# A mixture-of-experts stage: TensorE in program order, an overflow piece folded earlier, one product for a slot's token and weight

## The chip, the cores and the metric

The kernel runs on one core of a Trainium2 chip. Its engines are TensorE (PE in the profile, with PEld for the loading of its stationary operand), VectorE (DVE), ScalarE (ACT), GpSimd (POOL) and SyncE (SP). The metric is the device time of one execution in microseconds, lower is better; several executions are run and the median is taken.

## The reference

The model has two layers on 512 tokens of width 1024. Each layer has two attention mixers and a SwiGLU block. The block of the first layer is dense; that of the second is a mixture of 8 experts, two for each token:

```python
logits = (h @ w_router).astype(jnp.float32)
top_val, top_idx = lax.top_k(logits, TOP_K)            # TOP_K = 2, 8 experts
top_w = jax.nn.softmax(top_val, axis=-1)
combine = jnp.sum(jax.nn.one_hot(top_idx, N_EXPERTS) * top_w[..., None], axis=-2)
for e in range(N_EXPERTS):
    out = out + combine[..., e:e + 1] * swiglu(h, w_gu_e[e], w_dn_e[e])   # 1024 -> 2 x 1408 -> 1024
```

All is in float32. Only the expert block of the second layer is touched by the change.

## The kernel before

**Precision.** Each float32 operand of the large products is split into a high part (rounded) and a low remainder: for weights, ScalarE makes `ehi` (L1468) and VectorE subtracts it to give `elo` (L1469). A product then is three products on TensorE: high by high, high by low, low by high.

**The experts.** `moe` (L1706) runs the 8 experts one after the other. An expert has 128 slots for its tokens; where it got more, up to 64 more are kept as an overflow. The first expert to run is expert 0; the others follow in an order by their counts that is worked out on the chip (`rank`, L1228). With these inputs two of the eight have an overflow: the first and the fifth to run. All that belongs to an overflow stands under a branch, `self.over(e)`, that each engine takes or not by the expert's count.

**One expert**, `expert_blocks` (L1552), is a generator that is stepped once per k. It has four gate/up pieces u = 0 to 3 of 352 columns (8 k each, 6 products a k: L1647, L1648) and three down pieces d = 0 to 2 (11 k each, 3 products a k: L1681 to L1683). The loop counts them as (u, k) with u = 0 to 3 for gate/up and 4 to 6 for down. Around them stand, at places given by constants: the evacuation of a gate/up piece (`evac_gu`: Silu on ScalarE, a product on VectorE), the transposes of the activation (`tr`, L1577, then `ah` by L1581 and `al` by L1582), the weight splits (`SN`), and the scatter of the previous expert's rows (`rest`, at ER0).

**The overflow of an expert.** Ahead of each gate/up piece 32 products of the overflow rows (L1627, here called an overflow piece) go to two PSUM banks. They are folded by `ov_gu(u)`: two ScalarE copies (L1549), two VectorE adds (L1550), a Silu (L1590), a product (L1591). `OV` = 5 is the k of the pieces 0 to 2; the last is folded in the down piece d = 0 at `OV3` = 6. At `OT` = 8 the results are transposed (`ov_tr`, L1598) and split into `aot` (L1601, L1602), and behind d = 0 come 66 overflow down products (L1695, L1696).

**The slots of the next expert** are prepared meanwhile by `prep_a`, a generator too. It makes four one-hot matrices of tokens by slots (`one_hots`, L1274, on POOL; on VectorE for the first expert), multiplies them by the token numbers (`slots`, L1289) and by the weights (`slot_weights`, L1307), turns these into `ix` and `w` and gathers the rows (L1501). `prep_b` (at PB, PB1) transposes and splits the gathered rows, `prep_over` those of the overflow. For the first expert, `prep_a` also runs the rest of the routing (`route_rest`, 26 small VectorE operations and an exponential).

**What sets the order.** ScalarE issues in program order, by an order region around the whole kernel. On the other engines the compiler's scheduler chooses a fixed order from its own estimates of time, with the program order as priority. An instruction that finds its operands not ready holds up all that stands behind it on its engine.

Of the kernel before, what the change touches and what calls it, by code (L numbers as in the profile page):

```python
# [43 lines left out]
ER = 11  # L44
EA = 4
ORDER = (7, 3, 4, 5, 0, 6, 1, 2)
P0 = (0, 2), (0, 6), (1, 1)
OV, OV3, OT, OY = 5, 6, 8, (5, 8)
ER0 = 3
LA = 2  # L50
SN = (2, 4, 6, 8), (2, 4, 6, 8), (2, 4, 6, 8), (2, 4, 6), (7, 8, 9, 10), (1, 4, 8), (1, 4, 8)
TU, TE = 5, 6
TD = 5
PA, PA1, PA2, PB, PB1, PO = (1, 2), (2, 0), (2, 4), (4, 2), (4, 7), (5, 4)
FD = 3
PINH = ()
BK = 0, 1, 2, 3, 4, 5, 6, 7
# [19 lines left out]
class Trunk:  # L77
# [1129 lines left out]
    def route_rest(self):  # L1207

        nc, rp = self.nc, self.rp

        def over_e(a):
            return a.unsqueeze(2).to_broadcast([P, NT, NE])

        e2, w1 = rp.tile([P, NT], F32, name="e2"), rp.tile([P, NT], F32, name="w1")
        nc.vector.tensor_sub(e2, self.m8[:, :, 1], self.m8[:, :, 0])
        nc.scalar.activation(e2, e2, AF.Exp)
        nc.vector.tensor_scalar_add(w1, e2, 1.0)
        nc.vector.reciprocal(w1, w1)
        nc.vector.tensor_mul(e2, w1, e2)
        nc.vector.tensor_sub(self.M, self.M, self.s1)  # L1220
        nc.vector.tensor_tensor(self.s1, self.s1, over_e(w1), op=ALU.mult)
        nc.vector.tensor_tensor(self.M, self.M, over_e(e2), op=ALU.mult)
        nc.vector.tensor_add(self.wt, self.s1, self.M)
        self.rank()
        self.cols = rp.tile([P, NT, NE, 3], BF16, name="cols")
        self.weight_cols(self.cols, self.wtr, rp.tile([P, NT, NE], F32, name="wrem"))

    def rank(self):  # L1228
# [40 lines left out]
    def one_hots(self, n, pos, q):  # L1269

        oh = []
        for t in range(NT):
            o = self.ex.tile([P, CAP], BF16, tag="oh", bufs=4, name=self.nm("oh"))[:, :n]
            i = q.tensor_scalar(o, self.iotas[:, :n], pos[:, t], None, op0=ALU.is_equal)  # L1274
            self.tc.keep_in_program_order(i)
            oh.append(o)
        return oh

    def slots(self, n, oh):

# [205 lines left out]
    def prep_a(self, e):  # L1486

        nc, ex = self.nc, self.ex
        o = ORDER[e]
        oh = self.one_hots(CAP, self.posr[:, :, o:o + 1] if e else self.pos[:, :, 0:1], nc.gpsimd if e else nc.vector)  # L1490
        yield
        sl, fin = self.slots(CAP, oh)
        self.sl = sl
        if e:
            wfin = self.slot_weights(oh, sl, self.cols[:, :, o], self.psl)
            yield
        fin()
        g = self.g = [ex.tile([P, D], F32, tag="xg0", bufs=1, name=self.nm("xg")), self.views[-1]]

        def get(j):  # L1500
            nc.gpsimd.indirect_dma_start(out=g[j], out_offset=None, in_=self.hd[:, :],  # L1501
                                         in_offset=bass.IndirectOffsetOnAxis(ap=sl[j][2], axis=0))

        get(0)
        if e == 0:
            self.counts()
        self.ne[e] = nc.values_load(self.cnti[0:1, o:o + 1] if e else self.cnti[0:1, NE:], min_val=0, max_val=S)
        with self.over(e):
            get(1)
        if e == 0:  # L1510
            yield
            self.route_rest()
            yield
            wfin = self.slot_weights(oh, sl, self.cols[:, :, o])
            yield
        wfin()

    def prep_b(self):

# [32 lines left out]
    def expert_blocks(self, e, sl, xs, xo):  # L1552
# [51 lines left out]
        def ov_y(d):  # L1604
            c = dcol(d)
            self.fold(yo[:, c], ops[d][:, :c.stop - c.start], yo[:, c])
            nc.vector.tensor_scalar_mul(yo[:, c], yo[:, c], sl[1][3])

        def evac_gu(u, pg, pu):
            c = slice(u * GC, (u + 1) * GC)  # L1610
            nc.scalar.activation(a[:, c], pg, AF.Silu)  # L1611
            nc.vector.tensor_mul(a[:, c], a[:, c], pu)  # L1612
# [5 lines left out]
        last = None  # L1618
        for u in range(DFE // GC):
            ws = self.e_next(KD // GK)  # L1620
            with self.over(e):  # L1621
                for k in range(KD):
                    hi, lo = ws[k // GK]
                    st, sp, kk = k == 0, k == KD - 1, k % GK
                    for w, s0, s1 in ((hi, st, False), (lo, False, sp)):
                        for g in range(2):
                            nc.tensor.matmul(og[g], xo[:, k], w[:, g, kk], start=s0, stop=s1)  # L1627
            if u:
                evac_gu(u - 1, *last)
            last = pg, pu = self.psa()[:, :GC], self.psa()[:, :GC]  # L1630
            for k in range(KD):
                yield u, k
                if (u, k) == (0, ER0) and self.rest:
                    self.rest()
                if k == OV and u < 3:
                    with self.over(e):
                        ov_gu(u)
                if k == TU:
                    trev = tr(u * GC // P)
                if k in SN[u]:  # L1640
                    self.e_split()
                if k == TE:
                    trev()
                hi, lo = ws[k // GK]
                st, sp, kk = k == 0, k == KD - 1, k % GK
                for x, w, s0, s1 in ((xh, hi, st, False), (xh, lo, False, False), (xl, hi, False, sp)):
                    nc.tensor.matmul(pg, x[:, k], w[:, 0, kk], start=s0, stop=s1)  # L1647
                    nc.tensor.matmul(pu, x[:, k], w[:, 1, kk], start=s0, stop=s1)  # L1648
            self.e_splits(SN[u].count(KD))
        evac_gu(u, *last)  # L1650
        dws = []
        for d in range(ND):
            if d == 0:
                dws.append(self.e_next(3))
            if d != 1:
                py = self.psa()
            pd, py = py[:, :dcol(d).stop - dcol(d).start], None
            for k in range(KE):
                yield 4 + d, k
                if d == 0 and k == TD:  # L1660
                    tr(KE)()
                if k in SN[4 + d]:
                    self.e_split()
                if d == 0 and k == OV3:
                    with self.over(e):
                        ov_gu(3)
                if d == 0 and k == OT:
                    with self.over(e):
                        ov_tr()
                if d and k == 1:  # L1670
                    evac_y(d - 1, last)
                if (4 + d, k) == OY:
                    with self.over(e):
                        for j in range(ND):
                            ov_y(j)
                        nc.gpsimd.indirect_dma_start(out=self.out[0],
                                                     out_offset=bass.IndirectOffsetOnAxis(ap=sl[1][2], axis=0),
                                                     in_=yo, in_offset=None, compute_op=ALU.add)
                hi, lo = dws[d][k // DK]
                kk = k % DK  # L1680
                nc.tensor.matmul(pd, ah[:, k], hi[:, 0, kk], start=k == 0, stop=False)  # L1681
                nc.tensor.matmul(pd, ah[:, k], lo[:, 0, kk], start=False, stop=False)  # L1682
                nc.tensor.matmul(pd, al[:, k], hi[:, 0, kk], start=False, stop=k == KE - 1)  # L1683
            last = pd
            if d == 0:
                py = self.psa()
                dws += [self.e_next(3) for _ in range(ND - 1)]
                ops.append(self.psa())
                with self.over(e):  # L1689
                    for j, ws in enumerate(dws):  # L1690
                        ps = ops[j][:, :dcol(j).stop - dcol(j).start]
                        for k in range(KE):
                            hi, lo = ws[k // DK]
                            kk = k % DK
                            nc.tensor.matmul(ps, aot[:, k], hi[:, 0, kk], start=k == 0, stop=False)  # L1695
                            nc.tensor.matmul(ps, aot[:, k], lo[:, 0, kk], start=False, stop=k == KE - 1)  # L1696
# [9 lines left out]
    def moe(self):  # L1706
# [19 lines left out]
            self.e_load()  # L1726
        self.hold = False
        next(pb)
        xo = self.prep_over(0)
        self.e_splits(1 + LA)  # L1730
        for e in range(NE):
            sl = self.sl
            for u, k in self.expert_blocks(e, sl, self.xs, xo):
                if e == 0 and (u, k) in P0:
                    next(pa, None)
                if e + 1 == NE:
                    continue
                if (u, k) == PA:
                    pa = self.prep_a(e + 1)
                if (u, k) in (PA, PA1, PA2):  # L1740
                    next(pa, None)
                if (u, k) == PB:
                    pb = self.prep_b()
# [74 lines left out]
    def whole(self):  # L1818
# [14 lines left out]
        with order:  # L1833
# [15 lines left out]
                self.route()  # L1849
            with experts:  # L1850
                self.moe_pools(experts)
                self.moe()
                with tc.issue_after(self.last_dve.ins):
                    self.overflow_list()
        with ExitStack() as experts:
# [29 lines left out]
```

## Time and profile before

| What | Value |
|---|---|
| median of 3 runs | 1715.91 us (1715.15 to 1716.56) |
| the profiled execution | 1717.1 us |
| its span, first to last instruction | 1715.3 us |
| mean granted clock of TensorE | 0.985 of full speed |
| TensorE busy | 1644.6 us |
| VectorE, ScalarE, GpSimd busy | 1094.1, 978.3, 206.4 us |

The busy times are those of the page of the profile, and an engine is busy while one of its instructions runs. The granted clock is that of TensorE as the chip allowed it; it has two levels, 2.4 GHz (1.00) and 1.2 GHz (0.50). The expert stage takes the last third of the span.

### The profile page before, as it was taken

To read this page: it belongs to the slowest core of one execution; us is meant where nothing else is said; L and a number is where in the kernel's file an instruction comes from. 1 tells how busy PE (TensorE), PEld (TensorE's weight loads), DVE (VectorE), ACT (ScalarE), POOL (GpSimd) and SP (SyncE) were. 2 spreads that over 40 slices of the span, in tenths; PEclk is the share of its full clock that TensorE was granted. 3 is DMA by queue.
4 is the path that set the end of the run, shared out by engine and by line. 5 is a ranking of instruction groups with operands and counts; after the bars stand their busy time and mean duration, and the time that the engine had idled before them with its cause. 6 is when DMAs were issued, how large, how long until landed. Compare 5 with 4: busy or idle time off the path is not lost. (4 is left out here: it accounts for less than half of the span.)

```text
span 1715.3 us, 26180 instructions
## 1 busy us (share of the span) xinstructions
PE 1644.6 (96%) x9031; PEld 1433.5 (84%) x9031; DVE 1094.1 (64%) x1844; ACT 978.3 (57%) x1750; POOL 206.4 (12%) x315
## 2 busy tenths in 40 slices
PE   6989999999999999999989999999899999999996
PEld 6867987788888888888868987887789999999996
DVE  5578678765533332336578678655667888767984
ACT  5666589754422222324667589643656776656773
POOL 6112100002000000000122000101012202102200
PEclk9999999999999999999999999999799999999998
DMA  6333333235333332443433333352959999869993
GB/s 179 108 86 101 80 98 80 76 103 177 99 99 96 95 94 91 134 130 99 111 83 103 93 86 80 102 186 100 309 190 302 299 363 353 300 211 342 313 345 87
DMA packets 270840, 273.73 MB, mean 160 GB/s; under 512 B 11424, under 2 KB 259232, under 8 KB 270688
## 3 DMA queue, kind: packets, MB, share of 16 engines
q1 hardware_dynamic: 255936, 230.98, 42.7%
q0 software_dynamic: 12288, 37.40, 8.0%
q10 hardware_dynamic: 2464, 3.41, 0.6%
q8 instruction: 85, 1.39, 0.3%
q14 instruction: 67, 0.55, 0.1%
HBM read 250.21 MB, written 13.14 MB: 154 GB/s over the span
## 5 line engine op out<-in xcount | busy, mean ns | idle before, releaser
L320 PE MATMUL mm<-b,whi 128*128 128x512 f32 x1072 | 426.4, 398 | 4.1 <-DVE b L534 3.3
L322 PE MATMUL mm<-b,wlo 128*128 128x512 f32 x1072 | 419.5, 391 | 0.0
L321 PE MATMUL mm<-b,whi 128*128 128x512 f32 x1072 | 419.1, 391 | 0.0
L297 DVE TENSOR_TENSOR wlo<-wr,whi 128x1024 fp32r<-128x1024 f32 (+1 forms) x176 | 213.1, 1213 | 208.3 <-ACT whi L296 206.3
L296 ACT CAST whi<-wr 128x1024 fp32r<-128x1024 f32 (+1 forms) x176 | 182.9, 1042 | 262.9 <-issue 120.5
L1469 DVE TENSOR_TENSOR elo<-er,ehi 128x1408 fp32r<-128x1408 f32 (+3 forms) x200 | 305.1, 1568 | 26.0 <-ACT ehi L1468 15.5
L1468 ACT CAST ehi<-er 128x1408 fp32r<-128x1408 f32 (+3 forms) x200 | 256.1, 1324 | 22.3 <-DVE oh L1274 5.5
L320 PEld LDWEIGHTS mm<-b,whi 128*128 128x128 f32 x1072 | 201.8, 188 | 45.2 <-DVE b L534 4.6
L322 PEld LDWEIGHTS mm<-b,wlo 128*128 128x128 f32 x1072 | 201.3, 188 | 42.6 <-DVE wlo L297 0.4
L321 PEld LDWEIGHTS mm<-b,whi 128*128 128x128 f32 x1072 | 201.8, 188 | 39.1 <-issue 0.2
L356 PE MATMUL mm<-whi,b 128*128 128x256 f32 x320 | 92.3, 289 | 1.7 <-DVE b L532 1.1
L357 PE MATMUL mm<-wlo,b 128*128 128x256 f32 x320 | 91.3, 285 | 0.4 <-DVE wlo L297 0.4
L358 PE MATMUL mm<-whi,b 128*128 128x256 f32 x320 | 91.0, 285 | 0.0
L1682 PE MATMUL pa<-elo,ah 128*128 128x352 f32 (+1 forms) x264 | 85.8, 325 | 2.7 <-PEq L1621 0.3
L1683 PE MATMUL pa<-ehi,al 128*128 128x352 f32 (+1 forms) x264 | 84.7, 321 | 3.3 <-DVE al L1582 3.3
L1681 PE MATMUL pa<-ehi,ah 128*128 128x352 f32 (+1 forms) x264 | 86.5, 328 | 0.9 <-PEq L1689 0.2
L1647 PE MATMUL pa<-ehi,xh 128*128 128x352 f32 x256 | 85.8, 335 | 0.0
L1648 PE MATMUL pa<-elo,xh 128*128 128x352 f32 x256 | 83.7, 327 | 2.0 <-PEq L1621 0.5
L1648 PE MATMUL pa<-ehi,xl 128*128 128x352 f32 x256 | 83.1, 325 | 0.9 <-PEq L1621 0.3
L1647 PE MATMUL pa<-elo,xh 128*128 128x352 f32 x256 | 83.1, 325 | 0.3 <-DVE elo L1469 0.3
L1647 PE MATMUL pa<-ehi,xl 128*128 128x352 f32 x256 | 83.2, 325 | 0.0
L1648 PE MATMUL pa<-ehi,xh 128*128 128x352 f32 x256 | 83.1, 325 | 0.0
(351 smaller groups left out, 3107.6 us busy)
## 6 DMA issues: line engine op xcount, KB each, us to landing
er<-in_w_gu_exp_dram SPq DMA_DIRECT2D x248, 352.0 KB, 6.5
wr<-in_w_in_dram SPq DMA_DIRECT2D x80, 512.0 KB, 3.9
wr<-in_w_gu_dense_dram SPq DMA_DIRECT2D x44, 512.0 KB, 3.8
er<-in_w_dn_exp_dram SPq DMA_DIRECT2D x32, 704.0 KB, 10.6
wr<-in_w_dn_dense_dram SPq DMA_DIRECT2D x20, 512.0 KB, 3.4
er<-in_w_dn_exp_dram SPq DMA_DIRECT2D x16, 640.0 KB, 9.0
er<-in_w_dn_exp_dram SPq DMA_DIRECT2D x16, 528.0 KB, 10.2
b<-b POOLq DMA_DIRECT2D x64, 128.0 KB, 2.8
```

Source lines behind the costliest of these rows:

```text
L296: self.nc.scalar.copy(hi, raw)
L297: self.nc.vector.tensor_sub(lo, raw, f32v(hi))
L320: self.nc.tensor.matmul(ps, hi[:, j], hh[j], start=st, stop=False)
L321: self.nc.tensor.matmul(ps, hi[:, j], hl[j], start=False, stop=False)
L322: self.nc.tensor.matmul(ps, lo[:, j], hh[j], start=False, stop=sp)
L356: nc.tensor.matmul(o, a, hi[:, j], start=first, stop=False, skip_group_check=True)
L357: nc.tensor.matmul(o, a, lo[:, j], start=False, stop=False, skip_group_check=True)
L358: nc.tensor.matmul(o, b, hi[:, j], start=False, stop=last, skip_group_check=True)
L1468: self.nc.scalar.copy(hi, raw)
L1469: self.last_dve = self.nc.vector.tensor_sub(lo, raw, f32v(hi))
L1647: nc.tensor.matmul(pg, x[:, k], w[:, 0, kk], start=s0, stop=s1)
L1648: nc.tensor.matmul(pu, x[:, k], w[:, 1, kk], start=s0, stop=s1)
```

## The change

It has four parts, all in the expert stage.

1. Inside `moe` TensorE too issues in program order (a nested order region); before, the scheduler chose.
2. For every expert after the first, `slots_all` takes the place of `slots` and `slot_weights`: `cols` gets two more columns with the token number's two parts, and one product of five columns gives index and weight of a slot. Two reductions of VectorE make `ix` and `w` from it.
3. The folding of the last overflow piece moves from d = 0, k = 6 to u = 3, k = 5, and the overflow transposes from d = 0, k = 8 to k = 3.
4. For the first expert, the rest of the routing is issued ahead of its first block. Its overflow rows are transposed at (0,2) instead of ahead of the block, with two weight splits; its first overflow piece follows at (0,4), and is folded at k = 7. Its slot weights come at (2,0) and (2,2). The steps of `prep_a` for the second expert come at (1,2), (2,2) and (2,5), and for the later ones at (0,6), (1,4) and (2,0), where all had (1,2), (2,0) and (2,4).

```diff
-P0 = (0, 2), (0, 6), (1, 1)
-OV, OV3, OT, OY = 5, 6, 8, (5, 8)
+P0 = (2, 0), (2, 2)
+EO = 2
+OV, OT, OY = 5, 3, (5, 8)
...
-PA, PA1, PA2, PB, PB1, PO = (1, 2), (2, 0), (2, 4), (4, 2), (4, 7), (5, 4)
+PA = ((1, 2), (2, 2), (2, 5)), ((0, 6), (1, 4), (2, 0))
+PB, PB1, PO = (4, 2), (4, 7), (5, 4)
...
-        self.cols = rp.tile([P, NT, NE, 3], BF16, name="cols")
+        self.cols = rp.tile([P, NT, NE, 5], BF16, name="cols")
+        for j in range(2):
+            nc.gpsimd.tensor_copy(self.cols[:, :, :, 3 + j], self.tokc[:, :, j:j + 1].to_broadcast([P, NT, NE]))
...
+    def slots_all(self, n, oh, cols):
+
+        nc, ps, res = self.nc, self.psy(), []
+        for b in range(0, n, P):
+            m = min(P, n - b)
+            o = ps[:m, (b // P) * 8:(b // P) * 8 + 5]
+            for t in range(NT):
+                nc.tensor.matmul(o, oh[t][:, b:b + m], cols[:, t], start=t == 0, stop=t == NT - 1)
+            res.append([b, m] + [self.ex.tile([P, 1], d, tag=g, bufs=4, name=self.nm(g))[:m]
+                                 for d, g in ((I32, "ix"), (F32, "w"))])
+
+        def fin():
+            for b, m, ix, w in res:
+                o = ps[:m, (b // P) * 8:(b // P) * 8 + 5]
+                with nc.allow_low_precision(reason="whole numbers below 512"):
+                    nc.vector.tensor_reduce(ix, o[:, 3:5], axis=AX.X, op=ALU.add)
+                nc.vector.tensor_reduce(w, o[:, 0:3], axis=AX.X, op=ALU.add)
...
-        sl, fin = self.slots(CAP, oh)
+        sl, fin = self.slots_all(CAP, oh, self.cols[:, :, o]) if e else self.slots(CAP, oh)
         self.sl = sl
         if e:
-            wfin = self.slot_weights(oh, sl, self.cols[:, :, o], self.psl)
             yield
...
-        last = None
-        for u in range(DFE // GC):
-            ws = self.e_next(KD // GK)
+        def mm_over():
             with self.over(e):
                 for k in range(KD):
                     hi, lo = ws[k // GK]
...
+        last = None
+        for u in range(DFE // GC):
+            ws = self.e_next(KD // GK)
+            if (e, u) != (0, 0):
+                mm_over()
             if u:
                 evac_gu(u - 1, *last)
             last = pg, pu = self.psa()[:, :GC], self.psa()[:, :GC]
             for k in range(KD):
                 yield u, k
+                if (e, u, k) == (0, 0, EO):
+                    xo = self.prep_over(0)
+                    self.e_splits(LA)
+                if (e, u, k) == (0, 0, EO + 2):
+                    mm_over()
                 if (u, k) == (0, ER0) and self.rest:
                     self.rest()
-                if k == OV and u < 3:
+                if k == (OV if e or u else KD - 1):
                     with self.over(e):
                         ov_gu(u)
...
-                if d == 0 and k == OV3:
-                    with self.over(e):
-                        ov_gu(3)
...
-        xo = self.prep_over(0)
-        self.e_splits(1 + LA)
+        xo = None
+        self.e_splits(1)
+        next(pa)
+        p0 = pa
         for e in range(NE):
             sl = self.sl
             for u, k in self.expert_blocks(e, sl, self.xs, xo):
                 if e == 0 and (u, k) in P0:
-                    next(pa, None)
+                    next(p0, None)
                 if e + 1 == NE:
                     continue
-                if (u, k) == PA:
+                at = PA[min(e, 1)]
+                if (u, k) == at[0]:
                     pa = self.prep_a(e + 1)
-                if (u, k) in (PA, PA1, PA2):
+                if (u, k) in at:
                     next(pa, None)
...
-                self.moe()
+                with tc.manual_schedule(engines={mybir.EngineType.PE}):
+                    self.moe()
```

## Rows read from the trace of the kernel before

**Rows 1.** The page, part 1: busy time of an engine.

```profile
PE 1644.6 (96%) x9031; PEld 1433.5 (84%) x9031; DVE 1094.1 (64%) x1844; ACT 978.3 (57%) x1750; POOL 206.4 (12%) x315
```

**Rows 2.** Stages: length, busy time by engine (instructions), PEclk, DMA share, GB/s.

```profile
1210.00:1703.00 493.00, 479.63 (x3082) 461.90 (x3082) 370.23 (x391) 315.58 (x341) 74.00 (x45) 0.98 0.88 292
1280.00:1290.00 10.00, 9.42 (x38) 8.57 (x38) 6.55 (x8) 5.95 (x8) 0.00 (x0) 0.50 0.36 102
1524.40:1534.40 10.00, 9.21 (x61) 8.66 (x62) 7.85 (x8) 9.29 (x11) 0.00 (x0) 1.00 0.41 114
```

**Rows 3.** TensorE's waits in the expert stage: us in total, times, longest.

```profile
PE py L1527 <- DMA xg<-hd,ix: 5.6, 1, 5.6
PE pa L1683 <- DVE al L1582: 3.3, 2, 2.1
...
PE mm L1695 <- DVE aot L1602: 1.4, 2, 0.8
...
PE py L1289 <- POOL oh L1274: 0.7, 2, 0.5
...
PE py L1540 <- DMA ao<-hd,ix: 0.6, 1, 0.6
...
PE pa L1647 <- DVE elo L1469: 0.3, 1, 0.3
```

**Rows 4.** TensorE's timeline, third expert: start, us, operation, count.

```profile
1376.60 0.69 PE L1289 MATMUL py<-tokc,oh 128*128 128x1 bf16 x16
1377.23 0.48 PE L1307 MATMUL py<-cols,oh 128*128 128x3 bf16 x8
1377.64 0.43 PE L1647 MATMUL pa<-ehi,xh 128*128 128x352 f32 x1
```

**Rows 5.** TensorE's timeline, first expert, behind d = 0; idle time in brackets.

```profile
1279.70 0.50 PE L1683 MATMUL pa<-ehi,al 128*128 128x352 f32 x1 [2.11 <-DVE al L1582]
...
1284.20 0.63 PE L1695 MATMUL mm<-ehi,aot 128*128 128x352 f32 x1 [0.58 <-DVE aot L1602]
...
1290.19 0.32 PE L1695 MATMUL mm<-ehi,aot 128*128 128x352 f32 x1
```

**Rows 6.** The same places of the fifth expert.

```profile
1524.39 0.43 PE L1683 MATMUL pa<-ehi,al 128*128 128x352 f32 x1 [1.20 <-DVE al L1582]
...
1527.60 0.40 PE L1695 MATMUL mm<-ehi,aot 128*128 128x352 f32 x1 [0.79 <-DVE aot L1602]
...
1530.87 0.32 PE L1695 MATMUL mm<-ehi,aot 128*128 128x352 f32 x1
```

**Rows 7.** VectorE's timeline, first expert, d = 0.

```profile
1277.37 1.07 DVE L1550 TENSOR_TENSOR ao<-mm,ao 64x352 f32<-64x352 f32 x2 [1.30 <-ACT ao L1549]
1278.54 0.52 DVE L1591 TENSOR_TENSOR ao<-ao 64x352 f32<-64x352 f32 x1
1279.08 0.56 DVE L1582 TENSOR_TENSOR al<-py,ah 128x384 fp32r<-128x384 f32 x1
```

**Rows 8.** POOL's timeline: one-hots made while the first, third and fifth expert run.

```profile
1248.95 3.01 POOL L1274 TENSOR_SCALAR oh<-iotas,posr 128x192 bf16<-128x192 f32 x4 [40.94 <-PE py L1307]
...
1364.92 7.14 POOL L1274 TENSOR_SCALAR oh<-iotas,posr 128x192 bf16<-128x192 f32 x4
...
1471.59 6.19 POOL L1274 TENSOR_SCALAR oh<-iotas,posr 128x192 bf16<-128x192 f32 x4
```

**Rows 9.** ScalarE's timeline, first expert.

```profile
1222.98 1.38 ACT L1468 CAST ehi<-er 128x1408 fp32r<-128x1408 f32 x1 [0.58 <-DMA er<-in_w_gu_exp_dram]
...
1276.88 0.92 ACT L1549 COPY ao<-mm 64x352 f32<-64x352 f32 x2
```

**Rows 10.** VectorE's timeline, first expert: two of the routing's operations, a weight remainder.

```profile
1222.02 0.16 DVE L1217 TENSOR_SCALAR w<-e 128x4 f32<-128x4 f32 x1
...
1231.68 0.42 DVE L1250 TENSOR_TENSOR rt<-req,r_pos 128x256 f32<-128x256 f32 x1
1232.03 1.62 DVE L1469 TENSOR_TENSOR elo<-er,ehi 128x1408 fp32r<-128x1408 f32 x1
```

More of the change, by code (lines that the diff above doesn't have):

```diff
@@ L1277, in one_hots @@
         return oh
+    def slots_all(self, n, oh, cols):
[13 more added lines that the diff above has]
+                nc.vector.tensor_reduce(w, o[:, 0:3], axis=AX.X, op=ALU.add)
+        return res, fin
     def slots(self, n, oh):
@@ L1513, in prep_a @@
             yield
-            wfin = self.slot_weights(oh, sl, self.cols[:, :, o])
+            wfin = self.slot_weights(oh, sl, self.cols[:, :, o, 0:3])
             yield
-        wfin()
+            wfin()
     def prep_b(self):
@@ L1607, in ov_y @@
             nc.vector.tensor_scalar_mul(yo[:, c], yo[:, c], sl[1][3])
+        def mm_over():
+            with self.over(e):
+                for k in range(KD):
+                    hi, lo = ws[k // GK]
+                    st, sp, kk = k == 0, k == KD - 1, k % GK
+                    for w, s0, s1 in ((hi, st, False), (lo, False, sp)):
+                        for g in range(2):
+                            nc.tensor.matmul(og[g], xo[:, k], w[:, g, kk], start=s0, stop=s1)
         def evac_gu(u, pg, pu):
@@ L1620, in expert_blocks @@
             ws = self.e_next(KD // GK)
-            with self.over(e):
[L1622 to L1627, printed above, removed]
+            if (e, u) != (0, 0):
+                mm_over()
             if u:
@@ L1663, in expert_blocks @@
                     self.e_split()
-                if d == 0 and k == OV3:
-                    with self.over(e):
-                        ov_gu(3)
                 if d == 0 and k == OT:
```

## The prediction

> **What bounds the kernel now.** I read the page first, then the stages in equal windows, then TensorE's waits inside the expert stage, then the timeline of each place where it waits. TensorE (PE) is busy for 96% of the span [rows 1], and in the stretch from the first expert's gather to the last down product it is busy 479.6 of 493 us, at a mean granted clock of 0.98 [rows 2]. Nothing else comes near: VectorE has 370 us in that stretch, DMA a share of 0.88 [rows 2]. So this stage is a row of matrix products and ends later or earlier by exactly three things: products added or dropped, time in which PE waits, and time in which it runs at the lower clock. A faster transfer or a shorter copy is worth nothing unless it ends one of PE's waits.
>
> The table of waits [rows 3] gives the places. 5.6 us stand ahead of the first transposes, for the gather of the first expert's rows; the change leaves that chain as it is. 0.6 us more go to the overflow rows of that expert. 3.3 us go to `al` and 1.4 us to `aot`: both lie in the first down piece (d = 0) of an expert with more than 128 tokens. Of these there are two in the eight, the first and the fifth [rows 5, 6]. 0.7 us wait for POOL's one-hot rows and 0.3 us for one weight remainder, both while the first expert runs. The six experts without overflow show no wait worth a term, and there PE's order in the trace already follows the program's own, so fixing that order can only act in the first and the fifth.
>
> **The slot products.** For each expert after the first, 16 one-column products (L1289) and 8 three-column ones (L1307) become 8 five-column ones. In the third expert the 16 run from 1376.60 to 1377.23, so 0.63 us, and the 8 from 1377.23 to 1377.64, so 0.41 us [rows 4]. No row has five columns; the nearest is the 0.41 us of three, below which the new group will hardly go, and above it I allow 0.6 us. I take 0.41. The gain is 7 x 0.63 = 4.4 us (at 0.6 us each it would be 3.1). They sit between gate/up products on a PE that waits for nothing there, so this comes off the path whole. On VectorE two casts and two reductions become four reductions; nothing waits for them until the next expert's gather, which has two pieces of the expert to land.
>
> **The last overflow piece.** Now its folding (`ov_gu(3)`: two ScalarE copies, two VectorE adds, a Silu, a product) stands in d = 0 at k = 6, between the last transposes of the activation (k = 5) and the VectorE subtraction that makes `al`. The first expert shows it: VectorE does the adds from 1277.37, the product at 1278.54, and `al` only at 1279.08 [rows 7], while PE waits 2.11 us for that `al` and later 0.58 us for `aot` [rows 5]. The fifth expert repeats it with 1.20 and 0.79 us [rows 6]. Moved to k = 5 of u = 3 the folding has three k (18 products at 0.16 us, as 20 run from 1527.60 to 1530.87 [rows 6], so 2.9 us) and then the last piece's own work to hide in, and the operands of `aot` are transposed at k = 3 instead of 8, ahead of the last transposes. All four waits go: 2.11 + 0.58 + 1.20 + 0.79 = 4.7 us. What is late next is ScalarE's copy for `ah`, which now stands behind the two `aot` copies instead; those start some 1.5 us before it, so I leave nothing over. If that cover fails, one wait of about 1 us stays.
>
> There is a second price. Behind the 2.11 us wait the granted clock is 0.50 from 1280 to 1290, behind the fifth expert's 1.20 us it stays at 1.00 [rows 2]. The work between the end of the `al` wait and the 21st overflow down product is the same in both: 1279.70 to 1290.19 is 10.49 us, less the wait 9.91 [rows 5]; 1524.39 to 1530.87 is 6.48, less the wait 5.69 [rows 6]. The lower of the two levels, 1.2 GHz, cost 4.2 us. With the wait gone I count it back.
>
> **The start.** The overflow rows are now transposed behind two k of the first expert's own products instead of after four products. At the lower clock two k, 12 products of 0.29 us: 0.16 and 0.13 more (the 4.2 us above, over 27 products and 11 transposes), are some 3.5 us, and the rows came 0.6 us late, so the 0.6 us wait [rows 3] goes. Against it: the rest of the routing is issued ahead of the first block, and its 26 small VectorE operations, between 0.16 and 0.42 us each [rows 10], about 5 us, now compete with the subtraction that makes the overflow rows' remainder. Also the first folding comes at k = 7 behind three more weight copies, which still wait for their data (0.58 us at 1222.98 [rows 9]), with only four k (3.8 us) until the next overflow product wants its bank. The chain can begin behind the fourth weight remainder, some 3 us before the first overflow product wants that subtraction: the bounds are 0 and about 2.3 us, with the whole chain ahead of it. In the rows of before such chains are cut up between other operations, so I take 0.5 us.
>
> **Program order in the first expert.** The 0.7 + 0.3 us waits come from a written-out order that guessed the routing's end wrongly; they go with it, 1.0 us. But a new wait appears. The one-hot rows of the second expert need the buffers of the first's, and POOL started them only when the last L1307 of the first expert had read those, after 40.94 us of waiting [rows 8]. The change puts that L1307 at (2,0) and the second expert's slot products at (2,2): between them PE has 12 products, 1.9 us. POOL needs 3.01 us for four one-hots beside an idle VectorE and 6.19 to 7.14 beside a busy one [rows 8]. Formerly a whole overflow piece was run meanwhile; in program order that piece stands in front. The wait is the POOL time plus 0.1 less 1.9: from 1.2 to 5.3 us. Zero is excluded, as the buffers are four and all in use. VectorE at that point is folding, with one weight remainder; midway between 3.01 and 6.19 is 4.6 us, so 2.8 us of wait. The rows say that VectorE's load decides the size. The Trainium skill (SBUF — State Buffer, "Who interferes with whom") says which operations block GpSimd: a VectorE instruction with two SBUF inputs does, one that reads PSUM and SBUF doesn't. By it the folding's adds are harmless and one remainder (1.62) with one product (0.52) blocks: 3.01 + 2.14 + 0.1 - 1.9 = 3.3 us instead of 2.8, and the sum would be 0.5 us higher. That the other six runs of four one-hots, beside remainders, all take over 6 us agrees with it.
>
> For later experts the one-hots already start as soon as the previous expert's scatter has left POOL, in the third expert at 1364.92, and end 7.14 us later, at 1372.06 [rows 8]. The new place (1,4) comes 24 products and two transposes before 1376.60, some 4.3 us, so about 1372.3: ready by two tenths, nothing counted. The gather is issued four k earlier and is wanted two pieces later, as before. The SP loads keep their order.
>
> **The sum.** Gains 4.4 + 4.7 + 4.2 + 0.6 + 1.0 = 14.9; costs 2.8 + 0.5 = 3.3; net 11.6 us. The profiled execution took 1717.1 us, with a span of 1715.3 and 1.8 around it; it would be 1705.5. It lies 1.2 us above the median of 1715.91, so I predict 1704.3.
>
> **Rivals.** (a) The wait at the second expert's slot products drops the clock as the 2.11 us one did. For: 2.8 us is longer than it. Against: it is cut by single short products, and the full-rate overflow piece lies right before. Price 4.2 us more: 1708.5.
> (b) The move doesn't free `al`: the `aot` copies and subtractions take the place of the folding in front of it, and PE waits as before, with the clock. Against: the six experts with the same schedule and no folding show no such wait. Time 1704.3 + 3.3 + 4.2 = 1711.8, keeping the slot products and the `aot` wait.
> (c) Slower: in program order each overflow piece waits for the folding of the one before. There are six such places. From one overflow piece to the next lie 48 products, 7.7 us; a folding's two copies and two adds take about 1.6 us, from 1276.88 to 1278.44 [rows 7, 9], but queue behind two weight copies. It decides from three waits of over 2 us, each with 4.2 us of clock: three are 19 us, 1723. I see no queue that long.
> (d) More: the POOL rows come in 3.01 us (1.2 of wait) and the start costs nothing, and PE, no longer interrupted at the start, gets its full clock earlier, some 13 products at 0.13 us saved: 1704.3 - 1.6 - 0.5 - 1.7 = 1700.5.
>
> **How the numbers follow.** The sum 0.55, with its own range of 1702 to 1706.5; (a) 0.22; (b) 0.10; (c) 0.04; (d) 0.09. The range from 1700 to 1711 takes in the sum, (a) and (d), and the bounds of the POOL wait, and leaves (b) and (c) out. A change of 0.2%, 3.4 us, is about what a measurement here can tell from none, so faster means below 1712.5: the sum, (a), (d) and over half of (b), 0.90; same 0.06; slower 0.04.
>
> **What the profile will show.** Right: L1289 only for the first expert, 8 slot products an expert in about 0.4 us; no wait of PE for `al` or `aot`, and a clock of 1.00 through the end of the first expert; a wait for POOL's one-hots of 1 to 5 us at u = 2 of the first expert. Wrong: the clock low once more around that wait (a); `al` in the table of waits (b); waits of the overflow products for `ao` or for their banks (c). The sum is also wrong if the start of the first products moves, since 5.6 us of gather stand there that I left alone.

## The result, and the profile after

The changed kernel takes 1726.8 us (1725.75 to 1727.33, four executions), the kernel before 1716.0 us on the same chip: a ratio of 1.0063, 95% interval 1.0045 to 1.008. It is slower by 10.8 us where 11.6 us of gain were forecast. Its profiled execution took 1726.57 us with a span of 1724.7 us, at a mean granted clock of 0.982.

The page of the kernel after, part 1:

```profile
PE 1644.3 (95%) x8919; PEld 1435.0 (83%) x8919; DVE 1095.2 (64%) x1844; ACT 979.6 (57%) x1750; POOL 222.1 (13%) x317
```

TensorE issues 112 products fewer than in [rows 1], seven experts by 16, and is busy as long as before. Only POOL has grown by more than 2 us, by 15.7. The waits of TensorE in the expert stage of the kernel after (us in total, times, longest) say where the time is:

```profile
PE py L1290 <- POOL oh L1278: 11.4, 9, 2.2
PE py L1550 <- DMA xg<-hd,ix: 5.5, 1, 5.5
PE pa L1679 <- ACT am L1643: 4.4, 5, 1.0
...
PE py L1621 <- DVE xl L1553: 0.7, 2, 0.4
PE mm L1639 <- DVE ao L1573: 0.2, 1, 0.2
```

Against [rows 3], `al` and `aot` are gone, as meant. In their place stand 11.4 us for the one-hot rows, where there were 0.7, and five waits of nearly a microsecond at the first product of a gate/up piece. Three windows of the kernel after (columns as in [rows 2]):

```profile
1250.00:1260.00 10.00, 7.41 (x40) 7.19 (x41) 4.96 (x10) 3.52 (x4) 3.92 (x4) 0.83 0.72 225
1280.00:1290.00 10.00, 10.00 (x67) 10.00 (x65) 8.45 (x8) 9.25 (x10) 0.00 (x0) 1.00 0.55 176
...
1370.00:1380.00 10.00, 8.56 (x38) 8.12 (x38) 4.52 (x8) 3.47 (x5) 3.00 (x2) 0.66 1.06 372
```

The clock that was 0.50 from 1280 to 1290 is 1.00 now, but it falls in new places. One of them, the third expert in TensorE's timeline of the kernel after:

```profile
1367.53 0.20 PE L1290 MATMUL py<-cols,oh 128*128 128x5 bf16 x2
1369.88 0.18 PE L1290 MATMUL py<-cols,oh 128*128 128x5 bf16 x1 [2.15 <-POOL oh L1278]
1370.62 0.49 PE L1290 MATMUL py<-cols,oh 128*128 128x5 bf16 x5 [0.56 <-POOL oh L1278]
1371.04 0.66 PE L1679 MATMUL pa<-ehi,xh 128*128 128x352 f32 x1
1371.50 0.50 PE L1680 MATMUL pa<-ehi,xh 128*128 128x352 f32 x1
1371.79 0.50 PE L1679 MATMUL pa<-elo,xh 128*128 128x352 f32 x1
...
1377.84 0.32 PE L1680 MATMUL pa<-ehi,xl 128*128 128x352 f32 x1
1379.03 0.43 PE L1679 MATMUL pa<-ehi,xh 128*128 128x352 f32 x1 [0.87 <-ACT am L1643]
```

The slot product begins at 1367.53 with two of the four one-hots and waits for each of the others. Behind it 18 products start 0.29 us apart instead of 0.16, until 1376.92. And at 1379.03 comes the second kind of wait. POOL and VectorE in the same microseconds of the kernel after; the later POOL rows are the same four operations counted from the second and from the third on:

```profile
1358.49 2.20 POOL L1729 DMA_INDIRECT out_dram<-am,ix  x1 [39.34 <-ACT am L1648]
1360.16 10.40 POOL L1278 TENSOR_SCALAR oh<-iotas,posr 128x192 bf16<-128x192 f32 x4
...
1362.83 6.99 POOL L1278 TENSOR_SCALAR oh<-iotas,posr 128x192 bf16<-128x192 f32 x2
...
1366.31 4.26 POOL L1278 TENSOR_SCALAR oh<-iotas,posr 128x192 bf16<-128x192 f32 x2
...
1476.74 5.20 POOL L1278 TENSOR_SCALAR oh<-iotas,posr 128x192 bf16<-128x192 f32 x4
```

```profile
1354.52 7.76 DVE L1493 TENSOR_TENSOR elo<-er,ehi 128x1408 fp32r<-128x1408 f32 x5
1362.62 3.16 DVE L1493 TENSOR_TENSOR elo<-er,ehi 128x1408 fp32r<-128x1408 f32 x2 [0.34 <-DVEq L1668]
1365.69 0.51 DVE L1644 TENSOR_TENSOR am<-am,pa 128x352 f32<-128x352 f32 x1
1366.12 3.15 DVE L1493 TENSOR_TENSOR elo<-er,ehi 128x1408 fp32r<-128x1408 f32 x2
1371.15 0.16 DVE L1298 TENSOR_REDUCE ix<-py 128x1 int32<-128x2 f32 x1 [1.87 <-PE py L1290]
...
1478.88 1.07 DVE L1573 TENSOR_TENSOR ao<-mm,ao 64x352 f32<-64x352 f32 x2
```

The four one-hots need 10.40 us, where [rows 8] had 7.14: 2.73, 3.50, 3.52 and 0.76 us one by one. Each one gets done where VectorE's chain of weight remainders has a break: the first ends just behind the break before 1362.62, the second around the product at 1365.69, the last two after 1369.27, when VectorE is out of work. The fifth expert's four take 5.20 us, and there VectorE leaves its remainders at 1478.88 for adds that read PSUM. By the Trainium skill (SBUF — State Buffer, "Who interferes with whom") a VectorE instruction with two SBUF inputs contends with a GpSimd instruction that reads SBUF. These rows agree with it: beside remainders a one-hot took 2.73 to 3.52 us, with VectorE idle 0.76.

From the last activation transposes at (4,5) of one expert to those of the next, in us, worked out from the timelines (beside them two experiments, run 1 with the old places and run 11 with the three losses undone):

| From, to | before | after | run 1 | run 11 |
|---|---|---|---|---|
| 1st at | 1275.85 | 1278.54 | 1278.08 | 1271.53 |
| 1st to 2nd | 69.12 | 62.07 | 61.48 | 61.36 |
| 2nd to 3rd | 52.02 | 58.15 | 51.43 | 51.45 |
| 3rd to 4th | 51.98 | 58.23 | 51.37 | 51.50 |
| 4th to 5th | 71.53 | 72.13 | 72.04 | 72.14 |
| 5th to 6th | 65.09 | 62.07 | 61.22 | 61.43 |
| 6th to 7th | 52.11 | 56.83 | 51.37 | 51.49 |
| 7th to 8th | 50.46 | 50.49 | 50.50 | 50.59 |

The forecast's gains show behind the first expert's mark, 7.05 us, and behind the fifth's, 3.02. These two are rough, since the change moves work across the marks: the overflow transposes (1.36 and 0.82 us before) now lie ahead of them, and six down products more (0.96 us) behind the first. The third, fourth and seventh expert lose 6.1, 6.2 and 4.7 us: just the three whose one-hots took over 10 us.

### The profile page after: what moved, and what is told of

Same layout as the page of the kernel before. It is cut to its first block, busy times and chain, and to the rows that moved or that the text cites. A ratio compares the mean times of both kernels' runs of the same rounds, so it can differ in the third digit from the quotient of the medians.

```text
span 1724.7 us, 25976 instructions
## 1 busy us (share of the span) xinstructions
PE 1644.3 (95%) x8919; PEld 1435.0 (83%) x8919; DVE 1095.2 (64%) x1844; ACT 979.6 (57%) x1750; POOL 222.1 (13%) x317
## 5 line engine op out<-in xcount | busy, mean ns | idle before, releaser
L1679 PE MATMUL pa<-ehi,xh 128*128 128x352 f32 x256 | 90.2, 352 | 7.3 <-ACT am L1643 4.4
L1680 PE MATMUL pa<-ehi,xh 128*128 128x352 f32 x256 | 84.6, 330 | 0.0
L1680 PE MATMUL pa<-elo,xh 128*128 128x352 f32 x256 | 84.6, 330 | 0.0
L1680 PE MATMUL pa<-ehi,xl 128*128 128x352 f32 x256 | 84.4, 330 | 0.0
```

## The experiments

The first theory is that the new places of `prep_a` cost the time, with GpSimd's one-hots late and the clock falling behind them. The first rival is that the program order of TensorE costs it; the second that the waits at the first product of a piece are what the table calls them, waits for ScalarE's Silu. The time before was 1715.93 us beside the first four runs, 1715.57 beside the next four, 1715.62 beside the last three.

**1. The old places for the later experts.** One line of the changed kernel is edited:

```diff
-PA = ((1, 2), (2, 2), (2, 5)), ((0, 6), (1, 4), (2, 0))
+PA = ((1, 2), (2, 2), (2, 5)), ((1, 2), (2, 0), (2, 4))
```

> The changed kernel with the slot preparation of the later experts back at (1,2), (2,0), (2,4). Theory A (the one-hot rows of POOL are not ready at the new place (1,4), and the register load of the branch stands uncovered at (2,0)): the three waits for one-hots of the third, fourth and seventh expert (2.7 + 2.8 + 2.8 = 8.3 us) go, the products at the lower clock behind them (47 at 0.135 us, 6.3 us) go too, and five of the 0.87 us waits shrink to the 0.15 of the other branches (3.6 us): 1726.8 - 18.2 = about 1708.6. Theory B (program order on TensorE costs by itself, wherever the slots stand): the place matters little, above 1722.

Measured: 1705.22 us, ratio 0.9936 (0.9919 to 0.9952). One line turns 10.8 us of loss into 10.7 of gain, 3.4 us more than forecast (run 9 shows why part of it was missed). POOL, then TensorE, in the third expert of this kernel:

```profile
1359.11 11.69 POOL L1278 TENSOR_SCALAR oh<-iotas,posr 128x192 bf16<-128x192 f32 x4
```

```profile
1370.86 0.46 PE L1290 MATMUL py<-cols,oh 128*128 128x5 bf16 x8
```

The one-hots are even slower, but end at 1370.80, just ahead of the product. The wait is thus a matter of the distance between the scatter, behind which POOL makes them, and the product, and that distance is what the change had cut. Even here the one-hots end only 0.06 us ahead of it, and in run 8, at the same place, one product waits 0.3 us for them.

**2. Only the register load and gather back at (2,4).** At the third place of `prep_a` every engine also loads the expert's count into a register and branches on it (L1530, L1531).

```diff
-PA = ((1, 2), (2, 2), (2, 5)), ((0, 6), (1, 4), (2, 0))
+PA = ((1, 2), (2, 2), (2, 5)), ((0, 6), (1, 4), (2, 4))
```

> The changed kernel with only the third step (index, register load, gather) of the later experts moved from (2,0) back by four k to (2,4). Theory A: the five waits of 0.87 us at the start of u = 2 are TensorE's register load and branch, uncovered behind the untaken overflow branch; moved among products they shrink to 0.15 each: 3.6 us less, 1723.2, with the waits for one-hots as they were. Rival C (the table of waits is right, and u = 2 waits for the Silu of u = 1 to give its bank free): the waits stay, 1726.8.

Measured: 1721.42 us, ratio 1.0029 (1.0019 to 1.004), 5.4 us less than the changed kernel. Its ten executions spread from 1716.84 to 1722.78, and the table gave the load 4.4 us, so 5.4 is good to a microsecond or two. Its waits:

```profile
PE py L1290 <- POOL oh L1278: 11.4, 9, 2.3
PE py L1550 <- DMA xg<-hd,ix: 5.6, 1, 5.6
```

The waits for "ACT am" are gone though no Silu was moved, so the table's name was wrong. In the changed kernel the records of the two lines (duration in ns, start) show what TensorE's sequencer did between 1377.84 and 1379.03:

```profile
L1530 PEldq TENSOR_LOAD <-cnti x1: 313/313/313, 1378.4 to 1378.4; - x1
...
L1531 PEldq COMPARE_BRANCH  x1: 212/212/212, 1378.8 to 1378.8; - x1
```

At (2,0) the load follows directly on the branch of an overflow piece that isn't taken, and TensorE has nothing queued. At (2,4) it stood among products.

**3. Only the one-hots earlier.**

```diff
-PA = ((1, 2), (2, 2), (2, 5)), ((0, 6), (1, 4), (2, 0))
+PA = ((1, 2), (2, 2), (2, 5)), ((0, 1), (1, 4), (2, 0))
```

> The changed kernel with only the one-hots of the later experts issued at (0,1) instead of (0,6), ahead of the scatter of the expert before, slot products still at (1,4). Theory A: POOL starts them without waiting for that scatter, they are ready at (1,4): the three waits and the lower clock behind them go (8.3 + 6.3 us), the 0.87 us waits stay: about 1712.2. Theory B: above 1722.

Measured: 1710.5 us, ratio 0.9964 (0.995 to 0.9978), 16.3 us less than the changed kernel. POOL of this kernel now makes them ahead of the scatter, 48 us before the product at 1368.24 wants them:

```profile
1320.31 6.22 POOL L1278 TENSOR_SCALAR oh<-iotas,posr 128x192 bf16<-128x192 f32 x4 [0.68 <-DMA xg<-hd,ix]
...
1359.22 2.20 POOL L1729 DMA_INDIRECT out_dram<-am,ix  x1 [32.69 <-ACT am L1648]
```

The waits under the load's name stay (4.9 us in six; the sixth, of 0.46, stands at u = 1, where no load is issued, and in run 1 too). Those for the one-hots are left in the first expert alone (3.0).

**4. The changed kernel without TensorE's program order.**

```diff
-                with tc.manual_schedule(engines={mybir.EngineType.PE}):
-                    self.moe()
+                self.moe()
```

> The changed kernel with TensorE left to the scheduler, all else as changed. Theory A: in the experts without overflow the scheduler kept program order in the kernel before, so the slot products come at (1,4) and the waits for one-hots stay there: 1720 to 1728. Theory B: the order made the waits; without it the time falls below that of the kernel before, 1705 to 1713.

Measured: 1707.81 us, ratio 0.9953 (0.9937 to 0.997). By this number alone the order would be the culprit, and the first theory's forecast was missed. POOL's timeline of this kernel shows why:

```profile
1297.30 2.78 POOL L1278 TENSOR_SCALAR oh<-iotas,posr 128x192 bf16<-128x192 f32 x1
...
1323.06 3.71 POOL L1278 TENSOR_SCALAR oh<-iotas,posr 128x192 bf16<-128x192 f32 x1 [0.90 <-DMA xg<-hd,ix]
1358.62 2.30 POOL L1729 DMA_INDIRECT out_dram<-am,ix  x1 [31.85 <-ACT am L1648]
1360.41 6.37 POOL L1278 TENSOR_SCALAR oh<-iotas,posr 128x192 bf16<-128x192 f32 x3
```

Freeing TensorE's order changed POOL's: the scheduler put one of the four one-hots ahead of the scatter, and three beside the remainders end in time. (They also start nearer to a break of VectorE, see run 7.) The run took away the late one-hots as well as the order, so it doesn't tell the two apart.

**5 to 7. One part at a time on the kernel before.** Run 5 takes from the change only `slots_all` with the five columns, at the old places; run 6 only the move of the folding and of the overflow transposes; run 7 only the order region. Their edits, cut:

```diff
+            wfin = self.slot_weights(oh, sl, self.cols[:, :, o, 0:3])
+        sl, fin = self.slots_all(CAP, oh, self.cols[:, :, o]) if e else self.slots(CAP, oh)
...
-OV, OV3, OT, OY = 5, 6, 8, (5, 8)
+OV, OT, OY = 5, 3, (5, 8)
...
+                with tc.manual_schedule(engines={mybir.EngineType.PE}):
+                    self.moe()
```

> The kernel before with one part of the change alone: one product of five columns for index and weight, at the old places, TensorE left to the scheduler. The term of the prediction says 0.63 us for each of seven experts: 4.4 us less, 1711.5. Rival: five columns cost more than three and the scheduler re-orders, so less than half of it is seen, above 1713.7.

Measured: 1709.74 us, ratio 0.9967 (0.9954 to 0.9979). 5.8 us of gain for 4.4 in the sum, which the interval (3.6 to 7.9 us) takes in; its profiled execution also had 16 slow products behind the first expert's `al` wait instead of 24.

> The kernel before with one part alone: the last overflow piece folded at (3,5), the overflow transposes at d = 0, k = 3, TensorE left to the scheduler. The terms of the prediction say 4.7 us of waits for al and aot and 4.2 us of lower clock go: 1707. Rival: the scheduler, still guessing, puts the overflow transposes and the last transposes where their operands are late (the run without the order waited 2.1 us for al and 4.2 us for am and aot), and half or less of it is seen: above 1711.5.

Measured: 1713.96 us, ratio 0.999 (0.998 to 0.9999): 1.6 us, so the rival's forecast held. Two of its waits, and the window of the first expert's first down piece:

```profile
PE py L1577 <- DVE aot L1602: 2.5, 2, 1.3
PE pa L1680 <- DVE al L1582: 2.3, 1, 2.3
```

```profile
1280.00:1290.00 10.00, 8.67 (x46) 8.01 (x47) 7.08 (x8) 7.71 (x10) 0.00 (x0) 0.77 0.45 142
```

In this kernel the scheduler puts the overflow transposes (1279.92) ahead of the last transposes (1282.52), which so wait 1.19 us for `aot`; for `al` TensorE waits 2.33 us at the third product of a down step (L1680 here), and the clock still falls. The move does not free them by itself.

> The kernel before with one part alone: TensorE in program order, all places as before. Theory A (an order in program order costs where a step stands ahead of its operands): the slot weights of the first expert stand at (0,6), and the columns that they read were ready only 18 us later in the kernel before, so TensorE waits there for 10 us or more, with the lower clock behind it; the waits for al and aot stay: 1725 or more. Theory B' (program order is harmless or a gain): within 3 us of before.

Measured: 1719.67 us, ratio 1.0025 (1.0016 to 1.0035), 4.1 us slower, which lies between the two forecasts. Its waits, and two windows:

```profile
PE py L1307 <- DVE cols L1261: 6.7, 1, 6.7
...
PE py L1598 <- DVE al L1582: 3.1, 2, 1.6
PE mm L1627 <- DVE aot L1544: 1.5, 1, 1.5
```

```profile
1285.00:1290.00 5.00, 4.45 (x23) 4.38 (x24) 3.44 (x6) 4.80 (x6) 0.00 (x0) 0.66 0.02 5
1527.00:1532.00 5.00, 4.80 (x26) 4.74 (x27) 3.44 (x6) 4.45 (x6) 0.00 (x0) 0.68 0.02 5
```

With the old constants the first expert's slot weights stand at (0,6), 6.7 us before the routing has made them; the scheduler had simply run them later. In the experts without overflow the order costs next to nothing: 52.09 and 52.16 us for 52.02 and 51.98. But it does act there, on POOL. The third expert's one-hots in this kernel, and the break of VectorE's chain that comes next behind their start, in this kernel and (second) in the kernel before:

```profile
1367.10 11.69 POOL L1274 TENSOR_SCALAR oh<-iotas,posr 128x192 bf16<-128x192 f32 x4
```

```profile
1369.56 1.62 DVE L1469 TENSOR_TENSOR elo<-er,ehi 128x1408 fp32r<-128x1408 f32 x1 [0.34 <-ACT ehi L1468]
```

```profile
1365.85 3.16 DVE L1469 TENSOR_TENSOR elo<-er,ehi 128x1408 fp32r<-128x1408 f32 x2 [0.34 <-DVEq L1636]
```

The break begins 2.12 us behind the start here, 0.59 us behind it in the kernel before (1364.92), which is one remainder less. All kernels that make the four behind the scatter fall into these two groups (third, fourth and seventh expert, us, from the timelines):

| Kernels | TensorE's order | start to VectorE's next break | the four take |
|---|---|---|---|
| before, runs 5, 6, 10 | scheduler's | 0.57 to 0.60 | 7.13 to 7.16 |
| after, run 2 | program's | 2.11 to 2.13 | 10.40 to 10.42 |
| runs 1, 7, 8 | program's | 2.11 to 2.14 | 11.68 to 11.71 |

So the order made the one-hots slow, wherever the slot product stood, and the new place took away the slack that hid it. At the new place VectorE stands idle behind the late product, and the last one-hot takes 0.76 us instead of 2.04.

**8. Old places, and the first expert's slots a step earlier.** Run 1, and:

```diff
-P0 = (2, 0), (2, 2)
+P0 = (1, 6), (2, 0)
```

> The changed kernel with the later experts' slot preparation back at (1,2), (2,0), (2,4), and the first expert's slot weights at (1,6) and (2,0) instead of (2,0) and (2,2), so that POOL starts the second expert's one-hots some 8 us before their product at (2,2). Theory A: the last wait for one-hots (1.9 + 0.6 + 0.6 us) and 12 products at the lower clock (1.6 us) go: 4.7 us below the run with the old places, 1700.5. Rival: the columns of the weights are not ready at (1,6), and the wait only moves: 1704 to 1706.

Measured: 1700.24 us, ratio 0.9907 (0.9891 to 0.9924). A whole overflow piece now lies between the last reader of the first one-hots and the second expert's product, and POOL's 8.88 us fit in front of it, by 0.15 us (POOL, then TensorE, of this kernel):

```profile
1239.05 8.88 POOL L1278 TENSOR_SCALAR oh<-iotas,posr 128x192 bf16<-128x192 f32 x4 [31.40 <-PE py L1331]
```

```profile
1248.08 0.48 PE L1290 MATMUL py<-cols,oh 128*128 128x5 bf16 x8
```

**9. All places as changed, the one-hots on VectorE.**

```diff
-        oh = self.one_hots(CAP, self.posr[:, :, o:o + 1] if e else self.pos[:, :, 0:1], nc.gpsimd if e else nc.vector)
+        oh = self.one_hots(CAP, self.posr[:, :, o:o + 1] if e else self.pos[:, :, 0:1], nc.vector)
```

> The changed kernel with the one-hots of every expert made by VectorE instead of GpSimd; all places as in the changed kernel. Theory A (the slot product at (1,4) waits because GpSimd's four one-hots get through only in VectorE's gaps): VectorE makes them in its own queue, the waits for the one-hots (11.4 us in the changed kernel's table of waits) fall under 2 us and so do the slow products behind them (8 us), the waits for the register load stay: 1726.8 - 11.4 - 8 + up to 2 = about 1708. Rival (place (1,4) is too early whichever engine makes them, since VectorE's queue holds ten weight splits ahead of them): the waits stay and the time is above 1720.

Measured: 1703.41 us, ratio 0.9938 (0.9921 to 0.9954). No wait for one-hots is left, and the slow products behind them are gone; the waits for the load stay. VectorE makes the third expert's four in an eighth of the time that POOL needs in the changed kernel:

```profile
1355.75 1.24 DVE L1278 TENSOR_SCALAR oh<-iotas,posr 128x192 bf16<-128x192 f32 x4
```

So place (1,4) was never too early for TensorE. It was too early for GpSimd. The time is 4.6 us under the forecast of 1708, for two reasons that the traces show. A late product costs more than the table names: in the third expert of the changed kernel 3.51 us lie between the first slot product and the next gate/up product, here 0.40, so 3.11 more where the table has 2.15 + 0.56. Over the four places that is 1.6 us. And the profiled execution reached its first gate/up product at 1210.15 us, 2.1 us before that of the changed kernel; over all the traces but that of run 7 this start lies between 1210.07 and 1212.27, which the edits don't explain.

**10. Run 8 without the order region.**

> The kernel of the run with old places and the first expert's places one earlier (1700.2 us), without the region that keeps TensorE in program order. Theory A (the order is worth something once nothing waits in it, since it keeps the overflow pieces and their transposes where they were put): waits for al and aot come back and the clock falls behind them, 1704 to 1709. Rival (the order is worth nothing, the places alone bring the gain): 1699 to 1702.

Measured: 1706.33 us, ratio 0.9954 (0.9937 to 0.997). Its waits:

```profile
PE py L1600 <- DVE aot L1625: 2.5, 2, 1.3
PE pa L1712 <- DVE al L1605: 2.1, 1, 2.1
PE py L1600 <- DVE am L1644: 1.7, 1, 1.7
PE py L1600 <- PEq L1697: 1.6, 5, 0.4
```

Here the order is tested without the late one-hots. It is worth 6.1 us. Three of these waits are those that the move of the folding was to free; the fourth stands at the branch of the overflow transposes (L1697).

**11. The three losses undone, the slot product still at (1,4).** The changed kernel with

```diff
-P0 = (2, 0), (2, 2)
+P0 = (1, 6), (2, 0)
-PA = ((1, 2), (2, 2), (2, 5)), ((0, 6), (1, 4), (2, 0))
+PA = ((1, 2), (2, 2), (2, 5)), ((0, 1), (1, 4), (2, 4))
```

> The changed kernel with its slot product still at (1,4), its one-hots begun at (0,1), its register load at (2,4) and the first expert's slots and weights at (1,6) and (2,0). If the three losses are separate and complete, undoing each gives what it gave alone: 1726.8 - 16.3 (one-hots) - 5.4 (load) - 5.0 (first expert's places) = about 1700. If something else of the place (1,4) costs time, it stays above 1704.

Measured: 1699.8 us, ratio 0.9915 (0.9898 to 0.9931). The three add up (1726.8 - 16.3 - 5.4 - 5.0 = 1700.1), so no further loss of that size shows, though this execution too had an early start, at 1210.20. With run 8 it is the fastest version, some 15 us below the kernel before; the two can't be told apart.

## Why the prediction was wrong

**The step that failed** is the one on the later experts: "The new place (1,4) comes 24 products and two transposes before 1376.60, some 4.3 us, so about 1372.3: ready by two tenths, nothing counted." The distance was right: from the start of the one-hots to the product are 7.37 us after (1360.16 to 1367.53), 7.4 by the forecast. What was wrong is the 7.14 us, which was taken from [rows 8] as if it were the operation's own. It is how long VectorE's remainders let POOL through when POOL starts 0.59 us ahead of a break; starting 2.12 us ahead of one, the four took 10.40. What moved the start is part 1 of the change: with the order alone, at the old places, they take 11.69 (run 7). So the sentence "fixing that order can only act in the first and the fifth" failed with it: in the others the order changed next to nothing on TensorE, but it changed POOL's time. The same prediction bounded the first expert's four from 3.01 to over 6 us, said that VectorE's load decides, and then counted a margin of two tenths at nothing without a bound. Undone alone, this step gives 16.3 us back (run 3). In the third expert it is 5.8 us: 3.11 to the next gate/up product, and 2.7 over the 18 products and two transposes behind it, which take 5.88 us instead of the 3.20 of run 11.

**A thing overlooked** is the register load. "The SP loads keep their order" looked at the DMA queues of the moved step, not at what the step issues on TensorE itself. It costs 4.4 us by the table, 5.4 by the medians (run 2).

**Rival (a)**, that the clock falls behind the second expert's slot product, came true, with 12 slow products or 1.6 us rather than 4.2. The wait there, 3.0 us in the table, was forecast at 2.8. That is in part luck: POOL took 5.46 us where 4.6 were assumed, and with the small products between the waits 3.5 us were lost up to the next gate/up product. Both are gone in run 8, for 5.0 us.

**What held.** The gains were 14.9 us in the sum, which would give 1701.0 with no cost against them; with the three losses undone the kernel takes 1699.8. The eight five-column products take 0.40 us, the 16 others are gone. The waits for `al` and `aot` and the slow stretch behind the first went. In run 11 the way from the first gate/up product to the second mark of the table is 122.69 us for 133.10, 10.4 less where the terms that fall there (waits, clock, start, two slot products) make 9.75; the half microsecond counted against the start doesn't show. From the fourth mark to the sixth it is 3.05 us less for 1.20 + 0.79 + 2 x 0.63. All marks together give 15.0 us for the 14.9; the rest of what run 11 gained in its trace lies ahead of the first gate/up product, 1.7 us, and behind the last mark, 1.0, where nothing was forecast. But the prediction gave the end of the `al` and `aot` waits to the move alone; runs 6, 7 and 10 show that it takes the move and the order together. Rival (c), overflow pieces waiting for foldings, has 0.2 us in the table. The moved overflow transposes wait 0.7 us in two places, which the prediction put at nothing.

The account closes to a microsecond: -11.6 forecast, plus 16.3, 5.4 and 1.6, is +11.7, against a measured +10.8.

**What stays open.** That POOL's late one-hots cause the loss is shown (runs 3 and 9), and that the order lengthens them is shown by run 7 beside the kernel before. That VectorE's remainders are what holds POOL up is read from the timelines and the table at run 7; the contention by itself was not tried. Nor do the runs say why, with TensorE in program order, VectorE's chain stands one remainder later against the scatter.

## What to carry to other kernels

A duration on GpSimd beside a busy VectorE belongs to the place where it was read: when such work, its consumer or the order of another engine is changed, bound it anew. The longest row of the four, 7.15 us, would not have been enough here; the longest single one-hot of the third expert before, 3.42 us (1366.14 to 1369.56), taken four times gives 13.7, and all measured times lie below that. Count a margin smaller than the bound as a possible wait. When a step moves, list what it issues on every engine, registers and branches too, and look at what stands just ahead of it there. Here a fixed order paid only with places in which nothing waits: alone it cost 4.1 us, with the right places it gained 6.1.

## What the runs showed of the hardware

- Four one-hots of 128x192 take 3.01 us on POOL beside an idle VectorE [rows 8], 4.09 (run 3) to 11.71 us (run 1) beside its remainders, and 1.24 us on VectorE (run 9).
- A register load (0.31 us) and a branch on it (0.21 us) on TensorE, right behind a branch that isn't taken, leave 0.86 to 0.97 us without a product, in five places of the changed kernel. The table of waits names an engine for it that had long been done.
- The granted clock fell behind waits of 1.56 us (run 7: 0.66 and 0.68) and of 2.15 us and 0.56 us with one small product between (0.66), and stayed at 1.00 behind the 1.20 us of [rows 6]. Each time the products behind came at 0.29 us instead of 0.16 until the clock rose again, for 10 to 18 of them.
